# Moving the chunk borders of one token mixer and shortening two key blocks of the other, in a fused decoder block

## The chip, the cores and the metric

One core of a Trainium2 chip. The core has a matrix engine (TensorE, PE in the profile; its weight loads are PEld), a vector engine (DVE), an activation engine (ACT), GpSimd (POOL) and a queue engine for transfers (SP). The metric is device time in microseconds (us), the median of several runs; less is better.

## The reference

One decoder block on 16 learned meta tokens followed by 512 real tokens, model width 1024, 4 heads. All in float32. After a norm, one input projection feeds two token mixers that run side by side:

- Mixer 1 (mLSTM). Queries and keys go through a causal convolution and SiLU. Row j of the output is a sum over keys s <= j of exp(d[j,s]) (q_j . k_s) v_s, with d from running sums of gate logs, stabilised by a row maximum and divided by a normaliser.
- Mixer 2 (gated linear attention). A state S is carried over time, S_t = diag(alpha_t) S_(t-1) + k_t v_t^T, and o_t = S_t^T q_t, with a decay per key channel.

Each head's output is normed and gated, the two mixers are merged by sigmoid gates and projected, and a SwiGLU channel mixer follows. The meta rows are dropped at the end:

```
q_dec = q * exp(bc);  k_inv = k * exp(-bc);  k_end = k * exp(btot - bc)
att   = where(causal, q_dec @ k_inv.T, 0);   intra = att @ v
S_new = exp(btot)[:, None] * S + k_end.T @ v
out   = intra + q_dec @ S_prev               # per chunk; bc restarts in each
```

The chunk length is a choice of the implementation: any borders give the same sums.

## The kernel before

Activations lie transposed, channels on the 128 partitions and time along the free axis: 528 columns, the 16 meta tokens first. Weights come from memory in units of 128x1024 by the SP queue (some halves by POOL), through a ring of four raw buffers.

**fp32 by three fp32r products.** A float32 operand is split on chip into a high part rounded to fp32r (ACT, `whi`, L190) and the rest (DVE, `wlo`, L195), and a product becomes three: high x high, high x low, low x high (`mm3`, L304 to L306). The same is done for mixer 1's q, k, values and weights. Some projections are done in pairs by a seven-product scheme on 2x2 blocks (`seven`, L346 to L348), with additions on ACT and DVE in `sink_of` (L407 to L415). Mixer 2's own products are plain fp32: one instruction in the program, two records in the trace.

**Order.** The program writes the order of every engine's instructions by hand. `JOBS` lists the projection units. After each step of a unit (or every second one in a paired unit) `tick()` advances small generators, which issue the evacuations, the splits and the mixers' work between the products; `yield n` means "again in n ticks". One mixer head runs at a time. Each engine carries out its instructions in that order and waits when an operand is not there. Work tiles come from one pool of 60 buffers (`NTT`), PSUM tiles from 8 banks.

**Chunks.** Both mixers cut time into five windows of `CH` = 128 tokens that start with the meta tokens: the first holds 16 meta and 112 real tokens, the last only 16 real ones (`jrange`, `kwin`).

**Mixer 1, per head** (`mlstm`). For each key block i of the five, all queries from the block's first one on are scored at once, so that the blocks are 512, 400, 272, 144 and 16 queries wide: three fp32r products (L918 to L920) into a PSUM bank, an exponential on ACT, their product on DVE (L925), then a split of the result into `wh` (ACT, L935) and `wl` (DVE, L938) and a running sum (L942). Afterwards, for each of two 128-wide value halves, three products per block (L960 to L962) are accumulated into `num`. `values` first transposes v by TensorE (L755, L773), copies the result to a high part (L759, L776) and subtracts for a low part (L764, L781). `conv_act` makes the q and k splits (L737, L739).

**Mixer 2, per head** (`gla_decay`, `gla`, with `values` again, here without a low part). A running sum of the decay's logs, restarted at chunk borders by a 0/1 row `rmask` (L1006), gives the scaled q and k. Then four key windows are transposed (L1039), five score products are made (L1047), masked on DVE (L1050), eight products build the chunk states (L1058), ACT and DVE chain them (L1066 to L1071), and eighteen products give the output (L1079, L1081): ten with the masked scores, eight with the states.

`gate_rows` makes the gate logs and transposes them in 32-row pieces (L703). The epilogue of each head is `head_out`.

Of the kernel before, what the change touches and what calls it, by code (L numbers as in the profile page):

```python
# [15 lines left out]
P = 128  # L16
# [13 lines left out]
NCK = 5  # L30

# [71 lines left out]
def hybrid_block(ctx: ExitStack, tc: tile.TileContext, xT, wst, par, con, out):  # L103
# [526 lines left out]
    def gate_rows(ps):  # L630
# [45 lines left out]
        selector(0)  # L676

# [46 lines left out]
    def conv_act(q, k, src):  # L724
# [9 lines left out]
        for b, a in ((q, src[0].v), (k, src[1].v)):  # L734
            n = a.shape[1]
            hi, lo = tt(F32R, n), tt(F32R, n)
            act(hi, a, AF.Copy, scale=0.5)  # L737
            yield 2
            V.scalar_tensor_tensor(lo, a, 0.5, hi.bitcast(F32), ALU.mult, ALU.subtract)  # L739
            b.v = hi, lo  # L740
# [3 lines left out]
    def values(box, tail, vf, h, need_lo):  # L744
        dt = F32R if need_lo else F32
        full = []
        ps = []
        for vt in range(2):
            while vf[vt].v is None:
                yield 1  # L750
            yield 8 if h or not need_lo else 16
            f = vf[vt].v
            pb = bank()
            for c in range(4):
                T.transpose(pb[:, c * P:(c + 1) * P], f[:, c * CH:(c + 1) * CH], ident)  # L755
            yield 1
            ps.append(pb)
            a = tt(dt, NS)
            S.copy(a, pb)  # L759
            b = None  # L760
            yield 1
            if need_lo:
                b = tt(F32R, NS)
                V.tensor_tensor(b, pb, a.bitcast(F32), ALU.subtract)  # L764
            full.append((a, b))
            yield 1
        if h % 2 == 0:
            tail[0] = tt(dt, NS)
            tail[1] = tt(F32R, NS) if need_lo else None
        o = 256 * (h % 2)  # L770
        pb = bank()
        for vt in range(2):
            T.transpose(pb[:, vt * P:(vt + 1) * P], vf[vt].v[:, NT - CH:NT], ident)  # L773
        yield 1
        ta = tail[0][:, o:o + 256]
        S.copy(ta, pb[:, :256])  # L776
        tb = None
        yield 1
        if need_lo:
            tb = tail[1][:, o:o + 256]  # L780
            V.tensor_tensor(tb, pb[:, :256], ta.bitcast(F32), ALU.subtract)  # L781

        def pick(j):
            def f(c, vt):
                return full[vt][j][:, c * P:(c + 1) * P] if c < NCK - 1 else (ta, tb)[j][:, vt * P:(vt + 1) * P]
# [93 lines left out]
    WTOT = off  # L879
# [6 lines left out]
    def mlstm(h, q, k, v, gates, dst):  # L886
        while not gts.ready or q.v is None or k.v is None:
            yield 1
        (qh, ql), (kh, kl) = q.v, k.v
# [21 lines left out]
        for i in range(NCK + 1):  # L911
            cur = None
            if i < NCK:
# [3 lines left out]
                sp = bank()[:, :n]  # L917
                T.matmul(sp, kh[:, w0:w1], qh[:, j0:], start=True, stop=False)  # L918
                T.matmul(sp, kh[:, w0:w1], ql[:, j0:], start=False, stop=False)
                T.matmul(sp, kl[:, w0:w1], qh[:, j0:], start=False, stop=True)  # L920
                e = tt(n=n)
                cur = sp, e, WOFF[i], n
                act(e[:, :j1 - j0], dia[:, j0:j1], AF.Exp, bias=col(0, i))
            if prev:
                V.tensor_tensor(prev[1], prev[0], prev[1], ALU.mult)  # L925
            yield 1
# [6 lines left out]
            if prev:  # L933
                p, e_, o, m = prev
                S.copy(wh[:, o:o + m], e_)  # L935
            yield 1
            if prev:
                V.tensor_tensor(wl[:, o:o + m], e_, wh[:, o:o + m].bitcast(F32), ALU.subtract)  # L938
# [16 lines left out]
        for vt in range(2):  # L955
            for i in range(NCK):
                j0, o = jrange(i)[0], WOFF[i]
                n = NS - j0
                fi, la = i == 0, i == NCK - 1
                T.matmul(num[vt][:, j0:], vh(i, vt), wh[:, o:o + n], start=fi, stop=False)  # L960
                T.matmul(num[vt][:, j0:], vh(i, vt), wl[:, o:o + n], start=False, stop=False)  # L961
                T.matmul(num[vt][:, j0:], vl(i, vt), wh[:, o:o + n], start=False, stop=la)  # L962
# [17 lines left out]
    def gla_decay(h, gq, gk, dk):  # L980
# [27 lines left out]
        mid = CH // 2 - 1  # L1008
        c4 = 4 * CH
        v4 = lambda a: a[:, :c4].rearrange("p (a b) -> p a b", a=4)  # L1010
        V.tensor_tensor(v4(b3), v4(bc), v4(bc)[:, :, mid:mid + 1].to_broadcast([P, 4, CH]), ALU.subtract)
        V.tensor_scalar(b3[:, c4:], bc[:, c4:], bc[:, c4 + 7:c4 + 8], None, op0=ALU.subtract)
        ex = apool.tile([P, 3, 8], F32, tag="ex", name=nm("ex"), bufs=2)
# [8 lines left out]
        act(ex[:, 2, :4], b3[:, CH - 1:c4:CH], AF.Exp, scale=-1.0 / TAU)  # L1022
# [9 lines left out]
    def gla(h, dk, v, gates, dst):  # L1032
# [5 lines left out]
        for c in range(4):  # L1038
            T.transpose(pk[:, c * P:(c + 1) * P], ki[:, CH * c:CH * c + CH], ident)  # L1039
# [4 lines left out]
        for c in range(NCK):  # L1044
            j0, j1 = jrange(c)
            w0, w1 = kwin(c)
            T.matmul(ap_[:, j0:j1], ki[:, w0:w1], qd[:, j0:j1], start=True, stop=True)  # L1047
# [8 lines left out]
        for c in range(4):  # L1056
            for vt in range(2):
                T.matmul(Us[c // 2][:, 256 * (c % 2) + vt * P:256 * (c % 2) + (vt + 1) * P],  # L1058
                         kit[:, c * P:(c + 1) * P], gv(c, vt), start=True, stop=True)
            yield 1  # L1060
        Sv = None
        Sps = []
        for c in range(4):
# [7 lines left out]
            V.tensor_scalar(Sp, Sv, ex[:, 1, c + 1:c + 2], None, op0=ALU.mult)  # L1071
# [4 lines left out]
        for c in range(NCK):  # L1076
            j0, j1 = jrange(c)
            for vt in range(2):
                T.matmul(o[vt][:, j0:j1], gv(c, vt), att[:, j0:j1], start=True, stop=c == 0)  # L1079
                if c > 0:  # L1080
                    T.matmul(o[vt][:, j0:j1], Sps[c - 1][:, vt * P:(vt + 1) * P], qd[:, j0:j1],  # L1081
                             start=False, stop=True)
            yield 1
        yield 1
# [461 lines left out]
def _pack(inputs):  # L1546
# [63 lines left out]
    con[:, K_M01:K_M01 + NS] = keep  # L1610
# [21 lines left out]
```

## Time and profile before

| what | value |
|---|---|
| time, median of 3 runs | 938.07 us (938.03 to 938.1) |
| profiled execution: span, first to last instruction | 937.5 us |
| mean granted TensorE clock in it | 0.997 |
| TensorE busy, instructions | 914.6 us (98%), 6083 |
| DVE busy | 637.0 us (68%) |
| ACT busy | 536.2 us (57%) |
| POOL busy | 87.2 us (9%) |
| moved by transfers | 124.46 MB |

The page gives the profiled execution's span; the time of a run also holds what lies around the first and the last instruction, and here the median is 0.57 us above the span. A line of the page such as `L305 PE MATMUL b<-t,whi 128*128 128x512 f32` names the source line, the engine, the operation, the tile written and the tiles read, and the shapes: weights of 128x128, 512 columns streamed. In the timeline a row begins with the start and the duration in us, and ends with the count of instructions merged into it and, in brackets, how long the engine stood idle before it and what it waited for. Durations of products overlap, since a product starts while the one before it is still draining.

### The profile page before, as it was taken

The numbers are of one execution on the slowest core, as the hardware profiler recorded it, in microseconds if no ns is written. First come the engines' busy times: TensorE is split into PE (matmuls) and PEld (weight loads), VectorE is DVE, ScalarE is ACT, GpSimd is POOL, SyncE is SP. The second block draws the span as 40 slices with busy tenths as digits, with TensorE's granted clock in tenths as the row PEclk, the third lists the DMA queues.
The fourth block names the chain that finished last, engine by engine and source line by source line (L and its number), as shares of the span: only waits on it lengthen the run. The fifth ranks groups of instructions, "written<-read, shape, count | busy, mean of one in ns | idle before, by whom it ended". The sixth has DMA issues, their size and how long they took to land.

```text
span 937.5 us, 15478 instructions
## 1 busy us (share of the span) xinstructions
PE 914.6 (98%) x6083; PEld 839.7 (90%) x6083; DVE 637.0 (68%) x938; ACT 536.2 (57%) x956; POOL 87.2 (9%) x103
## 2 busy tenths in 40 slices
PE   6999999999999999999999999999999999999995
PEld 6988999989998899999998888889999999888885
DVE  6888886778865577777777556886676776932323
ACT  7666677888774166867674234443555555732322
POOL 0000022011100011111000000212111210000000
PEclk9999999999999999999999999999999999999998
DMA  6335475354652466565552344245777676332302
GB/s 254 114 115 165 141 167 123 71 141 110 159 155 90 113 162 162 133 135 142 123 147 90 113 139 134 87 121 116 192 174 201 176 180 169 114 104 76 113 1 90
DMA packets 48713, 124.46 MB, mean 133 GB/s; under 512 B 5376, under 2 KB 11520, under 8 KB 48640
## 3 DMA queue, kind: packets, MB, share of 16 engines
q1 hardware_dynamic: 35008, 101.32, 34.0%
q0 software_dynamic: 12544, 21.11, 14.6%
q8 instruction: 47, 0.77, 0.3%
q10 hardware_dynamic: 1088, 1.05, 0.3%
q14 instruction: 26, 0.21, 0.1%
HBM read 118.08 MB, written 5.37 MB: 132 GB/s over the span
## 4 chain that ended last, share of the span: by engine, by line
PE 84%; DVE 7%; ACT 6%; issue 2%; DMA 1%; SPq 0%; DVEq 0%; ACTq 0%
PE b L304 15%; PE b L305 15%; PE b L306 14%; PE b L346 11%; PE b L348 11%; PE b L347 11%; ACT t L134 2%; DVE wlo L195 2%; ACT whi L190 2%; PE b L1079 1%; DMA t<-xT 1%; PE b L1081 1%; PE b L1058 1%; ACT L133 1%; PE b L961 1%
## 5 line engine op out<-in xcount | busy, mean ns | idle before, releaser
L305 PE MATMUL b<-t,whi 128*128 128x512 f32 (+2 forms) x822 | 290.2, 353 | 1.3 <-DVE t L474 0.7
L304 PE MATMUL b<-t,whi 128*128 128x512 f32 (+2 forms) x774 | 273.9, 354 | 6.7 <-ACT t L134 6.7
L306 PE MATMUL b<-t,wlo 128*128 128x512 f32 (+2 forms) x774 | 270.9, 350 | 0.0
L195 DVE TENSOR_TENSOR wlo<-raw,whi 128x1024 fp32r<-128x1024 f32 x155 | 193.9, 1254 | 97.4 <-ACT whi L190 97.0
L346 PE MATMUL b<-t,whi 128*128 128x256 f32 (+1 forms) x864 | 248.7, 288 | 2.5 <-ACT t L407 1.2
L348 PE MATMUL b<-t,wlo 128*128 128x256 f32 (+1 forms) x864 | 244.5, 283 | 0.9 <-DVE wlo L195 0.9
L347 PE MATMUL b<-t,whi 128*128 128x256 f32 (+1 forms) x864 | 243.8, 282 | 0.0
L190 ACT CAST whi<-raw 128x1024 fp32r<-128x1024 f32 x155 | 161.9, 1048 | 55.2 <-PE b L347 22.7
L305 PEld LDWEIGHTS b<-t,whi 128*128 128x128 f32 x822 | 155.7, 189 | 24.1 <-DVE t L474 1.7
L304 PEld LDWEIGHTS b<-t,whi 128*128 128x128 f32 x774 | 146.9, 190 | 26.4 <-ACT t L134 6.7
L346 PEld LDWEIGHTS b<-t,whi 128*128 128x128 f32 x864 | 163.0, 189 | 3.7 <-ACT t L408 1.6
L306 PEld LDWEIGHTS b<-t,wlo 128*128 128x128 f32 x774 | 146.7, 190 | 20.0 <-DVE wlo L195 0.4
L348 PEld LDWEIGHTS b<-t,wlo 128*128 128x128 f32 x864 | 162.7, 188 | 1.7 <-DVE wlo L195 1.5
L347 PEld LDWEIGHTS b<-t,whi 128*128 128x128 f32 x864 | 163.0, 189 | 0.4
L134 ACT ACTIVATE t<-t 128x512 f32<-128x512 f32 (+6 forms) x140 | 80.4, 594 | 57.2 <-DVE t L1108 27.8
L185 POOL DMA_DIRECT2D raw<-wst x36 | 31.1, 864 | 361.7 <-DMA wf<-wst 94.0
L190 ACT CAST whi<-wf 128x1024 fp32r<-128x1024 f32 x36 | 37.8, 1049 | 22.4 <-PE b L347 12.6
L214 POOL DMA_DIRECT2D wf<-wst x36 | 34.8, 966 | 153.2 <-DMA wf<-wst 79.8
L134 ACT ACTIVATE t<-f 128x256 f32<-128x256 f32 (+1 forms) x24 | 11.6, 481 | 61.7 <-DVE f L1479 61.7
L195 DVE TENSOR_TENSOR wlo<-wf,whi 128x1024 fp32r<-128x1024 f32 x36 | 43.9, 1219 | 0.0
L1479 DVE TENSOR_TENSOR f<-f,b 128x512 f32<-128x512 f32 (+1 forms) x9 | 5.7, 629 | 53.8 <-PE b L306 53.8
L1401 ACT COPY t<-b 128x256 f32<-128x256 f32 x48 | 16.4, 374 | 44.3 <-PE b L348 44.3
(221 smaller groups left out, 1225.6 us busy)
## 6 DMA issues: line engine op xcount, KB each, us to landing
raw<-wst SPq DMA_DIRECT2D x155, 512.0 KB, 3.7
wf<-wst SPq DMA_DIRECT2D x36, 256.0 KB, 3.5
wf<-wst POOLq DMA_DIRECT2D x36, 256.0 KB, 5.9
raw<-wst POOLq DMA_DIRECT2D x36, 256.0 KB, 4.2
t<-xT SPq DMA_DIRECT2D x8, 264.0 KB, 6.9
pos<-t SPq DMA_DIRECT2D x8, 264.0 KB, 2.5
t<-xT SPq DMA_DIRECT2D x8, 256.0 KB, 3.9
t<-neg POOLq DMA_DIRECT2D x6, 272.0 KB, 6.4
```

Of the source, the lines that this page charges most:

```text
L134: S.activation(o, i, func, **kw)
L185: G.dma_start(lr(r, 0), lr(wst[v - 1], 0), accum_op=ALU.add)
L190: S.copy(t, src)
L195: V.tensor_tensor(t, src, hi.bitcast(F32), ALU.subtract)
L214: G.dma_start(lr(st.f, 1), lr(wst[u + 1], 1), accum_op=ALU.add)
L304: T.matmul(o, w_h, ah[:, c0:c1], start=first, stop=False)
L305: T.matmul(o, w_h, al[:, c0:c1], start=False, stop=False)
L306: T.matmul(o, w_l, ah[:, c0:c1], start=False, stop=last)
L346: T.matmul(o, h, xh_[k][:, c0:c1], start=start and k == 0, stop=False, skip_group_check=not start)
L347: T.matmul(o, h, xl_[k][:, c0:c1], start=False, stop=False, skip_group_check=not start)
L348: T.matmul(o, l, xh_[k][:, c0:c1], start=False, stop=k == 3, skip_group_check=not start)
L1401: s7=lambda: S.copy(s[:, lo], bz), s1=lambda: S.copy(s[:, hi], bx), s2=lambda: S.copy(r[:, lo], bx),
```

## The change

Mixer 2 gets chunk borders after the 16 meta tokens: one chunk of 16 meta keys, which have no real queries and only give a first state, and four chunks of 128 real tokens. Its values are transposed in windows that begin at token 16, plus one window of 16 meta tokens for both value halves, which lands on 16 partitions. The first state is one product with 16 rows and 256 columns; the scores are four products of 128 columns, the output sixteen (each of eight blocks by its scores and by its state). `rmask` is rewritten for these borders behind its last use by mixer 1's gates, and the mask of mixer 2 becomes four triangles.

Mixer 1 keeps its windows. Its last two key blocks (144 and 16 queries) are scored by one fp32 product each of the unsplit q and k, into one shared PSUM bank; their weights are not split, and each goes into `num` by one fp32 product with unsplit values. The first three blocks stay as they were. The unsplit q and k are twice the split ones, so a factor 0.25 is put into the DVE product.

```diff
+NWH = 3
@@ gate_rows
         selector(0)
+        G.memset(rmask[:, CH:NT:CH], 1.0)
+        G.memset(rmask[:, NM:NS:CH], 0.0)
@@ conv_act
-            b.v = hi, lo
+            b.v = hi, lo, a
@@ values
+        nw, w = (NWH, 0) if need_lo else (4, NM)
+        rest = [(c, vt) + kwin(c) for c in range(nw, NCK) for vt in range(2)] if need_lo else [
+            (None, vt, 0, NM) for vt in range(2)]
+        m = rest[0][3] - rest[0][2]
-            for c in range(4):
-                T.transpose(pb[:, c * P:(c + 1) * P], f[:, c * CH:(c + 1) * CH], ident)
+            for c in range(nw):
+                T.transpose(pb[:, c * P:(c + 1) * P], f[:, w + c * CH:w + (c + 1) * CH], ident)
-            a = tt(dt, NS)
-            S.copy(a, pb)
+            a = tt(dt, nw * P)
+            S.copy(a, pb[:, :nw * P])
-                V.tensor_tensor(b, pb, a.bitcast(F32), ALU.subtract)
+                V.tensor_tensor(b, pb[:, :nw * P], a.bitcast(F32), ALU.subtract)
-        for vt in range(2):
-            T.transpose(pb[:, vt * P:(vt + 1) * P], vf[vt].v[:, NT - CH:NT], ident)
+        for i, (c, vt, w0, w1) in enumerate(rest):
+            T.transpose(pb[:m, i * P:(i + 1) * P], vf[vt].v[:, w0:w1], ident)
-        S.copy(ta, pb[:, :256])
-        if need_lo:
-            V.tensor_tensor(tb, pb[:, :256], ta.bitcast(F32), ALU.subtract)
+        S.copy(ta, pb[:m, :n])
@@ mlstm
+                if i < NWH:
                     ...
+                else:
+                    if i == NWH:
+                        spn, en = bank(), tt()
+                    c = slice(WOFF[i] - WTOT, WOFF[i] - WTOT + n)
+                    sp, e = spn[:, c], en[:, c]
+                    T.matmul(sp, kf[:, w0:w1], qf[:, j0:], start=True, stop=True)
+            elif prev:
+                V.scalar_tensor_tensor(prev[1], prev[0], 0.25, prev[1], ALU.mult, ALU.mult)
+                if o < WTOT:
+                    S.copy(wh[:, o:o + m], e_)
+                if o < WTOT:
+                    V.tensor_tensor(wl[:, o:o + m], e_, wh[:, o:o + m].bitcast(F32), ALU.subtract)
+                if i >= NWH:
+                    T.matmul(num[vt][:, j0:], vh(i, vt), en[:, o - WTOT:o - WTOT + n], start=False, stop=i == NCK - 1)
+                    continue
@@ gla_decay
-        mid = CH // 2 - 1
+        mid = NM + CH // 2 - 1
     ...
-        act(ex[:, 0, :4], bc[:, CH - 1:c4:CH], AF.Exp, scale=-1.0 / TAU)
-        act(ex[:, 1, :4], bc[:, mid:c4:CH], AF.Exp, scale=-1.0 / TAU)
-        act(ex[:, 1, 4:5], bc[:, c4 + 7:c4 + 8], AF.Exp, scale=-1.0 / TAU)
+        act(ex[:, 0, 1:], bc[:, NM + CH - 1:NT - CH:CH], AF.Exp, scale=-1.0 / TAU)
+        act(ex[:, 1], bc[:, mid:NT:CH], AF.Exp, scale=-1.0 / TAU)
@@ gla
-            T.transpose(pk[:, c * P:(c + 1) * P], ki[:, CH * c:CH * c + CH], ident)
+            w = max(0, NM + CH * (c - 1))
+            T.transpose(pk[:, c * P:(c + 1) * P], ki[:, w:w + CH], ident)
-        for c in range(NCK):
-            T.matmul(ap_[:, j0:j1], ki[:, w0:w1], qd[:, j0:j1], start=True, stop=True)
+        for c in range(4):
+            T.matmul(ap_[:, blk(c)], ki[:, NM + CH * c:NM + CH * c + CH], qd[:, blk(c)], start=True, stop=True)
-        for c in range(4):
+        T.matmul(Us[0][:, :256], kit[:NM, :P], gv(None, 0), start=True, stop=True)
+        for c in range(3):
             for vt in range(2):
-                T.matmul(Us[c // 2][:, 256 * (c % 2) + vt * P:256 * (c % 2) + (vt + 1) * P],
-                         kit[:, c * P:(c + 1) * P], gv(c, vt), start=True, stop=True)
+                o = 256 * ((c + 1) % 2) + vt * P
+                T.matmul(Us[(c + 1) // 2][:, o:o + P], kit[:, (c + 1) * P:(c + 2) * P], gv(c, vt), start=True, stop=True)
-        for c in range(NCK):
+        for c in range(4):
             for vt in range(2):
-                T.matmul(o[vt][:, j0:j1], gv(c, vt), att[:, j0:j1], start=True, stop=c == 0)
-                if c > 0:
-                    T.matmul(o[vt][:, j0:j1], Sps[c - 1][:, vt * P:(vt + 1) * P], qd[:, j0:j1],
-                             start=False, stop=True)
+                T.matmul(o[vt][:, blk(c)], gv(c, vt), att[:, blk(c)], start=True, stop=False)
+                T.matmul(o[vt][:, blk(c)], Sps[c][:, vt * P:(vt + 1) * P], qd[:, blk(c)], start=False, stop=True)
```

The counts of `yield` along each path are the same as before, so everything keeps its place in the order of the ticks.

More of the change, by code (lines that the diff above doesn't have):

```diff
@@ L762, in values @@
             if need_lo:
-                b = tt(F32R, NS)
-                V.tensor_tensor(b, pb, a.bitcast(F32), ALU.subtract)
+                b = tt(F32R, nw * P)
+                V.tensor_tensor(b, pb[:, :nw * P], a.bitcast(F32), ALU.subtract)
             full.append((a, b))
             yield 1
[L767 to L770, printed above, removed]
+        n = len(rest) * P
+        if need_lo or h % 2 == 0:
+            tail[0] = tt(n=NS)
+        o = 0 if need_lo else n * (h % 2)
         pb = bank()
-        for vt in range(2):
-            T.transpose(pb[:, vt * P:(vt + 1) * P], vf[vt].v[:, NT - CH:NT], ident)
+        for i, (c, vt, w0, w1) in enumerate(rest):
+            T.transpose(pb[:m, i * P:(i + 1) * P], vf[vt].v[:, w0:w1], ident)
         yield 1
-        ta = tail[0][:, o:o + 256]
-        S.copy(ta, pb[:, :256])
-        tb = None
+        ta = tail[0][:m, o:o + n]
+        S.copy(ta, pb[:m, :n])
         yield 1
-        if need_lo:
-            tb = tail[1][:, o:o + 256]
-            V.tensor_tensor(tb, pb[:, :256], ta.bitcast(F32), ALU.subtract)
+        at = {r[:2]: i * P for i, r in enumerate(rest)}
         def pick(j):
             def f(c, vt):
-                return full[vt][j][:, c * P:(c + 1) * P] if c < NCK - 1 else (ta, tb)[j][:, vt * P:(vt + 1) * P]
+                if c is None:
+                    return ta
+                if (c, vt) in at:
+                    return ta[:, at[c, vt]:at[c, vt] + P]
+                return full[vt][j][:, c * P:(c + 1) * P]
             return f
@@ L878, in hybrid_block @@
         off += NS - jrange(i)[0]
-    WTOT = off
+    WTOT = WOFF[NWH]
     def selector(h):
@@ L888, in mlstm @@
             yield 1
-        (qh, ql), (kh, kl) = q.v, k.v
+        (qh, ql, qf), (kh, kl, kf) = q.v, k.v
         yield 6
@@ L916, in mlstm @@
                 n = NS - j0
[L917 to L921, printed above, removed]
+                if i < NWH:
+                    sp = bank()[:, :n]
+                    T.matmul(sp, kh[:, w0:w1], qh[:, j0:], start=True, stop=False)
+                    T.matmul(sp, kh[:, w0:w1], ql[:, j0:], start=False, stop=False)
+                    T.matmul(sp, kl[:, w0:w1], qh[:, j0:], start=False, stop=True)
+                    e = tt(n=n)
+                else:
[4 more added lines that the diff above has]
+                    T.matmul(sp, kf[:, w0:w1], qf[:, j0:], start=True, stop=True)
                 cur = sp, e, WOFF[i], n
                 act(e[:, :j1 - j0], dia[:, j0:j1], AF.Exp, bias=col(0, i))
-            if prev:
+            if prev and i <= NWH:
                 V.tensor_tensor(prev[1], prev[0], prev[1], ALU.mult)
+            elif prev:
+                V.scalar_tensor_tensor(prev[1], prev[0], 0.25, prev[1], ALU.mult, ALU.mult)
             yield 1
@@ L1609, in _pack @@
     con[:, K_MADD:K_MADD + NS] = np.where(keep, 0.0, -1e30)
-    con[:, K_M01:K_M01 + NS] = keep
+    con[:, K_M01:K_M01 + NS] = np.arange(P)[:, None] <= np.arange(NS)[None, :] % CH
     for h in range(H):
```

28 lines of the change are left out of this document (11 added, 17 removed).

## The prediction

> **What bounds the kernel now.** I read the page first (busy times, then the chain of work that ended last), then TensorE's own waits in order of time, then the instructions of the two mixers product by product.
>
> ```profile
> span 937.5 us, 15478 instructions
> PE 914.6 (98%) x6083; PEld 839.7 (90%) x6083; DVE 637.0 (68%) x938; ACT 536.2 (57%) x956; POOL 87.2 (9%) x103
> PE 84%; DVE 7%; ACT 6%; issue 2%; DMA 1%; SPq 0%; DVEq 0%; ACTq 0%
> ```
>
> TensorE (PE) is busy for 914.6 of 937.5 us, and 84% of the chain that ended last is its own work. So the time moves by what the change takes from or adds to TensorE, unless it makes TensorE wait. The timeline of TensorE has only a handful of waits between its first product and its last; the four inside mixer 1 that bear on the change (the bracket gives the idle time and what ended it):
>
> ```profile
> 73.32 0.50 PE L918 MATMUL b<-t,t 128*128 128x512 f32 x1 [0.63 <-DVE t L764]
> 102.77 0.47 PE L960 MATMUL b<-wh,t 128*128 128x512 f32 x1 [0.31 <-DVE t L764]
> 207.27 0.39 PE L346 MATMUL b<-t,whi 128*128 128x256 f32 x1 [1.24 <-ACT t L407]
> 213.13 0.39 PE L346 MATMUL b<-t,whi 128*128 128x256 f32 x1 [1.06 <-ACT t L408]
> ```
>
> What a product costs TensorE must be read from how far apart products start; the durations in the rows overlap.
>
> **Part A: mixer 1, key blocks 3 and 4 (144 and 16 queries wide) as single fp32 products.** There are three such groups per head: the scores, and the value product for each of the two value halves. Each was two blocks of three fp32r products. The tail of one value product in head 0, and the projection behind it:
>
> ```profile
> 99.70 0.23 PE L960 MATMUL b<-wh,t 128*128 128x144 f32 x1
> 99.76 0.28 PE L961 MATMUL b<-wl,t 128*128 128x144 f32 x1
> 99.87 0.27 PE L962 MATMUL b<-wh,t 128*128 128x144 f32 x1
> 99.99 0.22 PE L960 MATMUL b<-wh,t 128*128 128x16 f32 x1
> 100.06 0.26 PE L961 MATMUL b<-wl,t 128*128 128x16 f32 x1
> 100.17 0.26 PE L962 MATMUL b<-wh,t 128*128 128x16 f32 x1
> 100.28 0.37 PE L304 MATMUL b<-t,whi 128*128 128x264 f32 x1
> 100.49 0.28 PE L305 MATMUL b<-t,whi 128*128 128x264 f32 x1
> ```
>
> From 99.70 to the second projection product at 100.49 are 0.79 us. One 264-wide product takes 0.12 in a dense run (60.65 to 60.77 for the same form, below), so the six narrow ones cost 0.67, or 0.11 each, and 16 columns cost as much as 144. What is paid is not the columns but one load of 128x128 weights per product.
>
> Next, what a single fp32 product costs. In the trace one fp32 product is two records. Four 16-wide fp32 products of mixer 2 in a row (two rows left out), and the projection behind them:
>
> ```profile
> 289.45 0.29 PE L1079 MATMUL b<-t,t 128*128 128x16 f32 x2
> ...
> 290.04 0.38 PE L1081 MATMUL b<-t,Sp 128*128 128x16 f32 x2
> 290.26 0.48 PE L304 MATMUL b<-t,whi 128*128 128x512 f32 x1
> 290.58 0.39 PE L305 MATMUL b<-t,whi 128*128 128x512 f32 x1
> 290.81 0.40 PE L306 MATMUL b<-t,wlo 128*128 128x512 f32 x1
> ```
>
> 290.58 - 289.45 is 1.13; less 0.23 for one 512-wide product it is 0.90 for four, 0.22 each: two loads at 0.11. Up to 128 columns the price is the same, as L1058 in the chain of waits shows: two 128-wide products (four records) in 0.45. L1500 there prices a wide product, and L755 the transposes of part C:
>
> ```profile
> 85.66 0.44 PE b L755 x4
> ...
> 270.42 0.45 PE b L1058 x4
> ...
> 916.50 0.43 PE b L1500 x2
> ```
>
> L1500 is one fp32 product 256 wide: 0.43. Its columns are the cost there, so 144 columns take 0.43 x 144/256 = 0.24. A group of 0.67 becomes 0.24 + 0.22 = 0.46 and saves 0.21. Twelve groups: **-2.5 us**. The bounds: six loads against four alone (0.67 - 0.44) would give 0.23 per group, -2.8; if the 144-wide one cost as much as the 256-wide, 0.02, or -0.2.
>
> The Trainium skill speaks against this part: FP8 and Floating Point Precision, TensorE Precision Notes, has true fp32 make four passes through the array, and three fp32r products are three. By passes alone a group would rise from 3 x 160 to 4 x 160 columns, at 0.12/264 us a column 0.07 us more, and part A would be +0.9 instead of -2.5. The rows show the four passes on wide products (0.43 for 256 columns against 0.12 for 264 in fp32r) but a floor per load on narrow ones, so I take the rows.
>
> With part A also go, per head, the splits of blocks 3 and 4 on ACT (L935) and DVE (L938), one DVE split of the values' tail (L781) and a quarter of the two others (L764). They are off TensorE's path except at the waits above; see part D.
>
> **Part B: mixer 2 with four full blocks.** Scores go from 5 products to 4, the output from 18 to 16. Removed are three narrow fp32 products per head (widening 112 to 128 columns is free, as the load is the price): 3 x 0.22 x 4 heads = **-2.7 us**. The price is measured in this very form; were only the columns paid, it would be 3 x 0.03 x 4, -0.3, the upper bound.
>
> **Part C: what the 16 meta keys cost.** The state of the meta chunk is one fp32 product with 16 rows and 256 columns in place of two 128-wide ones: 0.43 against 0.44, equal. Two of the ten value transposes per head now have 16 columns instead of 128; they cost 0.11 (L755 above, four in 0.44). But both kinds use only a corner of the array, and the trace has one such place, the gate transposes with 32 rows. One of them, then (from another window) five in a row:
>
> ```profile
> 60.65 0.28 PE L305 MATMUL b<-t,whi 128*128 128x264 f32 x1
> 60.77 0.28 PE L306 MATMUL b<-t,wlo 128*128 128x264 f32 x1
> 60.98 0.24 PE L703 MATMUL b<-pr,t 32*128 32x32 f32 x1
> 61.15 0.39 PE L304 MATMUL b<-t,whi 128*128 128x264 f32 x1
> 61.38 0.29 PE L305 MATMUL b<-t,whi 128*128 128x264 f32 x1
> ```
>
> ```profile
> 55.75 0.28 PE L306 MATMUL b<-t,wlo 128*128 128x264 f32 x1
> 55.96 0.49 PE L703 MATMUL b<-pr,t 32*128 32x32 f32 x5
> 56.61 0.28 PE L305 MATMUL b<-t,whi 128*128 128x264 f32 x1
> ```
>
> 60.77 to 61.38 is 0.61; less two wide products (0.24) one transpose costs 0.37. With five it is 0.86 - 0.24 = 0.62. Four more cost 0.25, 0.06 each, so 0.31 us is the price of going into the small form and out again: the load of the next weights is not started until the work before it has ended.
>
> The Trainium skill has the rule: TensorEngine Tiling (Array Packing), Tiling Modes, Key Properties, says that "Mode switching requires drain", and lists both 32 rows and 32 columns as modes. The row agrees for rows; no row shows columns.
>
> Per head: the 16-row product enters and leaves once, +0.31 - 0.01 = +0.30; the two narrow transposes (adjacent) once, +0.31, their own price left at 0.11. I take both, as L703 is the only narrow form there is: 4 x 0.61 = **+2.4 us**. Bounds: below, no break for either and 0.06 per transpose, -0.06 - 0.4 = -0.5; above, twice the break (0.62, if the wide fp32 product or a full array drains longer than a 32-wide one), +4.9.
>
> **Part D: the waits.** L764 now writes 384 columns instead of 512. By form:
>
> ```profile
> L764 DVE TENSOR_TENSOR t<-b,t 128x512 fp32r<-128x512 f32 x8 | 5.5, 688 | 5.2 <-ACT t L759 5.2
> L938 DVE TENSOR_TENSOR wl<-t,wh 128x400 fp32r<-128x400 f32 x4 | 2.3, 575 | 5.2 <-ACT wh L935 5.2
> ```
>
> 113 ns for 112 columns, so 128 columns are 0.13: the waits at 73.32 and 102.77 shorten by 0.13 each, **-0.3** (0 if TensorE's earlier work, not DVE's length, set them). Before the wait at 213.13 ACT does this:
>
> ```profile
> 211.46 1.15 ACT L134 ACTIVATE t<-t 128x512 f32<-128x512 f32 x2
> 212.51 0.29 ACT L935 CAST wh<-t 128x144 fp32r<-128x144 f32 x1
> 212.71 0.36 ACT L408 COPY t<-b 128x256 f32<-128x256 f32 x1
> ```
>
> L935 for block 3 is gone, L408 comes 0.2 earlier. But head 3's score group saves its 0.2 between the two ACT waits and only waits longer: **0** in sum.
>
> Costed at nothing: the two strided memsets on POOL (used 9%; the next reader is mixer 2), the block 3 evacuation that now shares a PSUM bank with block 4 (DVE's product for block 3 is issued behind block 4's scores anyway), the ACT copy of the tail (512 columns instead of 256, but the two copies ahead of it are 128 shorter each). If that cover were gone, each would cost at most one instruction of 0.2 to 0.6 us per head. No DMA is added or moved.
>
> **Sum**: -2.5 - 2.7 + 2.4 - 0.3 = -3.1; as parts A and B lose a little where ACT or DVE lead (head 3's 0.2 is already out), I take **-2.9**. Span 937.5 - 2.9 = 934.6. The median of the runs shown is 938.07, 0.57 above the span; **935.2 us**.
>
> **Rivals.** *No break* (932.3 to 934): if neither narrow form breaks the run, part C is -0.5 and the sum -2.5 - 2.7 - 0.5 - 0.3 = -6.0, 932.1; if only the transposes don't, -4.2, 933.9. For: 32 output columns are unseen. Against: L703.
>
> *Swallowed* (937.3): ACT, not TensorE, is the bound up to 213 us, and what part A saves before it (all but the two value groups of head 3, 10/12 of 2.5 = 2.1) becomes longer waits at 207 and 213: -2.9 + 2.1 = -0.8. For and against stand in ACT's rows:
>
> ```profile
> 190.13 0.37 ACT L776 CAST t<-b 128x256 fp32r<-128x256 f32 x1 [1.57 <-PE b L773]
> 193.50 0.37 ACT L410 COPY t<-b 128x256 f32<-128x256 f32 x1 [0.17 <-PE b L348]
> ```
>
> Only 0.17 us of slack at 193.50, but 1.57 before 190.13, ended by TensorE: if TensorE is early there, so is ACT. The weights' splits could still lag.
>
> *Four passes* (938.5): part A as +0.9; sum +0.9 - 2.7 + 2.4 - 0.3 = +0.3. Needs the floor per load not to hold, which the six products contradict.
>
> *Slower: buffers.* The pool of work tiles has 60 buffers. The unsplit q and k, so far free once their low parts are made, must now live until block 4's scores, and the weights of blocks 3 and 4 until the last value product. For head 3:
>
> ```profile
> 176.15 0.70 DVE L739 SCALAR_TENSOR_TENSOR t<-t,t 128x528 fp32r<-128x528 f32 x1
> 208.23 0.26 PE L920 MATMUL b<-t,t 128*128 128x16 f32 x1
> ```
>
> That is 208.5 instead of 176.9, 32 us with two buffers fewer. If the pool runs out, an ACT instruction between 193 and 208 stands still until 208.5, with the projection's copies and splits behind it; one that is due at 204.1 (ACT's gate functions start there) waits 4.4 us, and TensorE with it: 935.2 + 4.4 = 939.6. With the same in one more head, 944.0. It decides from 2.9 + 1.9 = 4.8 us of added waits. Against: no wait in the trace can be named as one for a buffer, and the values' tail takes one buffer less per head pair.
>
> **Chances.** What a measurement of this kernel can tell from no change is about 0.2%, 1.9 us. Forecast 0.50, no break 0.18, swallowed 0.18, four passes 0.05, buffers 0.09. Faster by over 0.2% (below 936.2): the first two, 0.68. Within: 0.23. Slower: 0.09. The range 932.4 to 938.0 leaves out the lowest end of *no break* and the slower cases.
>
> **What would show it.** In the profile after: the TensorE records of blocks 3 and 4 as four loads in 0.46 us; TensorE's busy time about 3 us lower; a gap of 0.1 us before and 0.2 behind the 16-row product and the narrow transposes, or none (then 932 to 934); the waits at 207 and 213 of the old size. Wrong would be: waits of TensorE on ACT or DVE in heads 1 to 3 longer by more than 1 us, or single fp32 products that start over 0.3 us apart.

## The result, and the profile after

| | before | after |
|---|---|---|
| time, median | 938.09 us (938.03 to 938.54) | 933.33 us (933.12 to 933.61) |
| profiled execution: span | 937.5 us | 931.8 us |
| TensorE busy, instructions | 914.6 us, 6083 | 910.6 us, 6027 |
| DVE busy | 637.0 us | 633.5 us |
| ACT busy | 536.2 us | 534.0 us |

The ratio of the times is 0.9947, 95% interval 0.9935 to 0.9959: the changed kernel is faster by 4.8 us. The forecast was 935.2 in a range from 932.4 to 938.0. The spans differ by 5.7 us, more than the times: in all later runs the time is 1.7 to 2.1 us above the span, while the kernel before's median is only 0.57 above the span of its profiled execution, so that this execution was itself, as far as these gaps tell, some 1.2 us longer than the median. That excess lies ahead of the mixers: the product behind TensorE's wait near 70 us starts at 70.00 us there and between 68.22 and 68.95 in the traces of all the other runs. Effects are therefore compared below by the times, or within one stage.

From the page of the kernel after: span, busy times, and the shares of the chain that ended last.

```profile
span 931.8 us, 15342 instructions
PE 910.6 (98%) x6027; PEld 834.4 (90%) x6027; DVE 633.5 (68%) x926; ACT 534.0 (57%) x944; POOL 87.2 (9%) x105
PE 83%; DVE 8%; ACT 6%; issue 2%; DMA 1%; SPq 0%; DVEq 0%; ACTq 0%
```

TensorE has 56 records fewer and is busy 4.0 us less; the bound has not moved. Line numbers have: `mm3` is L305 to L307 now, `seven` L347 to L349, mixer 1's scores L925 to L927 and L934, its value products L980 to L982 and L978.

A single fp32 group in head 0 (one value half's two last blocks; four records in one row), with what stands before and behind it, from TensorE's timeline after:

```profile
97.46 0.29 PE L982 MATMUL b<-wh,t 128*128 128x272 f32 x1
97.58 0.54 PE L978 MATMUL b<-t,t 128*128 128x144 f32 x4
97.97 0.37 PE L305 MATMUL b<-t,whi 128*128 128x264 f32 x1
98.18 0.28 PE L306 MATMUL b<-t,whi 128*128 128x264 f32 x1
```

98.18 - 97.58 is 0.60; less one 264-wide product (0.12) the group costs 0.48. Predicted were 0.46 after 0.67. The 144-wide product by itself stands among the scores of head 1:

```profile
122.93 0.28 PE L307 MATMUL b<-t,wlo 128*128 128x264 f32 x1
123.05 0.41 PE L934 MATMUL b<-t,t 128*128 128x144 f32 x2
123.20 0.38 PE L305 MATMUL b<-t,whi 128*128 128x264 f32 x1
123.42 0.29 PE L306 MATMUL b<-t,whi 128*128 128x264 f32 x1
```

123.42 - 123.05 less 0.12 is 0.25, where the prediction had 0.24 by its columns.

The two narrow transposes of a head's values (L778, 16 columns), same view:

```profile
260.65 0.28 PE L349 MATMUL b<-t,wlo 128*128 128x256 f32 x1
260.77 0.38 PE L778 MATMUL b<-pr,t 128*16 128x128 f32 x2
260.91 0.36 PE L347 MATMUL b<-t,whi 128*128 128x256 f32 x1
261.11 0.28 PE L348 MATMUL b<-t,whi 128*128 128x256 f32 x1
```

They start without a gap, 0.12 behind the product before them, and 261.11 - 260.77 less one 256-wide product (0.12) leaves 0.22 for two. There is no break.

The 16-row product (L1074) and the two 128-wide ones behind it (L1078):

```profile
265.13 0.28 PE L349 MATMUL b<-t,wlo 128*128 128x256 f32 x1
265.34 0.69 PE L1074 MATMUL b<-t,t 16*128 16x256 f32 x2
265.96 0.71 PE L1078 MATMUL b<-t,t 128*128 128x128 f32 x4
266.43 0.37 PE L347 MATMUL b<-t,whi 128*128 128x256 f32 x1
```

Here the run is broken: 0.21 from the product before to L1074 where dense products stand 0.12 apart, then 0.62 where a 256-wide fp32 product takes 0.43. The break is there for the 16-row product and not for the transposes with 16 columns. The weight loads (PEld) say the same: the load for the transposes starts 0.10 us ahead of its product (260.77), while behind the 16-row product the next load starts only with its own product, after 0.33 us without any:

```profile
260.67 0.19 PEld L778 LDWEIGHTS b<-pr,t 128*16 128x16 f32 x2
265.96 0.52 PEld L1078 LDWEIGHTS b<-t,t 128*128 128x128 f32 x4 [0.33 <-issue]
```

Not every form with fewer rows breaks the run. Two products with 96 rows start 0.13 us behind the one at 210.94, and the next follows at 211.31, 0.12 for each:

```profile
211.07 0.41 PE L1010 MATMUL b<-t,a2s 96*128 96x264 f32 x2
```

Mixer 2's output, 16 single fp32 products in place of 18 (first and last, and the projection behind):

```profile
280.95 0.38 PE L1098 MATMUL b<-t,t 128*128 128x128 f32 x2
...
282.50 0.39 PE L1099 MATMUL b<-t,Sp 128*128 128x128 f32 x2
282.65 0.48 PE L305 MATMUL b<-h,whi 128*128 128x512 f32 x1
282.97 0.40 PE L306 MATMUL b<-t,whi 128*128 128x512 f32 x1
```

282.97 - 280.95 less 0.23 is 1.79 for the eight shown, 0.22 each at 128 columns, the price that 16 columns had before.

The waits of TensorE in mixer 1, first the one of the kernel before that the prediction did not show, then those over 0.2 us of the kernel after:

```profile
70.00 0.50 PE L894 MATMUL b<-t,sel 128*128 128x512 f32 x1 [1.07 <-ACT acol L697]
```

```profile
68.94 0.50 PE L900 MATMUL b<-t,sel 128*128 128x512 f32 x1 [0.85 <-ACT acol L700]
100.88 0.47 PE L980 MATMUL b<-wh,t 128*128 128x512 f32 x1 [0.73 <-DVE t L769]
191.18 0.39 PE L349 MATMUL b<-t,wlo 128*128 128x256 f32 x1 [0.34 <-DVE wlo L196]
203.33 0.38 PE L347 MATMUL b<-t,whi 128*128 128x256 f32 x1 [0.57 <-ACT t L408]
208.78 0.38 PE L347 MATMUL b<-t,whi 128*128 128x256 f32 x1 [0.72 <-ACT t L409]
```

Before, they sum to 4.31 us (1.07 and the four in the prediction), after to 3.21. The wait ahead of head 0's first score product (73.32 before) is gone, that at 207.27 has halved, that at 213.13 lost a third, and a new one of 0.34 has come. The wait near 70 us differs from trace to trace, whatever the kernel (0.57 to 1.07 in the others), so its 0.2 is not put down to the change.

### The profile page after: what moved, and what is told of

It is laid out like the page before. It is cut to its first block, busy times and chain, and to the rows that moved or that the text cites. A ratio compares the mean times of both kernels' runs of the same rounds, so it can differ in the third digit from the quotient of the medians.

```text
span 931.8 us, 15342 instructions
## 1 busy us (share of the span) xinstructions
PE 910.6 (98%) x6027; PEld 834.4 (90%) x6027; DVE 633.5 (68%) x926; ACT 534.0 (57%) x944; POOL 87.2 (9%) x105
## 4 chain that ended last, share of the span: by engine, by line
PE 83%; DVE 8%; ACT 6%; issue 2%; DMA 1%; SPq 0%; DVEq 0%; ACTq 0%
PE b L305 14%; PE b L306 14%; PE b L307 14%; PE b L349 12%; PE b L347 12%; PE b L348 12%; ACT t L135 3%; DVE wlo L196 2%; ACT whi L191 2%; DMA t<-xT 1%; PE b L1099 1%; PE b L1098 1%; PE b L1078 1%; ACT L134 1%; PE b L761 1%
## 5 line engine op out<-in xcount | busy, mean ns | idle before, releaser
L305 PE MATMUL b<-t,whi 128*128 128x512 f32 (+2 forms) x774 | 274.1, 354 | 6.6 <-ACT t L135 6.6
L307 PE MATMUL b<-t,wlo 128*128 128x512 f32 (+2 forms) x774 | 270.8, 350 | 0.0
L347 PE MATMUL b<-t,whi 128*128 128x256 f32 (+1 forms) x864 | 248.5, 288 | 1.6 <-ACT t L409 1.0
L349 PE MATMUL b<-t,wlo 128*128 128x256 f32 (+1 forms) x864 | 244.7, 283 | 0.8 <-DVE wlo L196 0.8
L305 PEld LDWEIGHTS b<-t,whi 128*128 128x128 f32 x774 | 146.7, 190 | 26.1 <-ACT t L135 6.6
L347 PEld LDWEIGHTS b<-t,whi 128*128 128x128 f32 x864 | 163.2, 189 | 3.0 <-ACT t L409 1.7
L307 PEld LDWEIGHTS b<-t,wlo 128*128 128x128 f32 x774 | 146.6, 189 | 20.0 <-DVE wlo L196 0.3
L349 PEld LDWEIGHTS b<-t,wlo 128*128 128x128 f32 x864 | 162.6, 188 | 1.5 <-DVE wlo L196 1.4
```

Of the source, the lines that this page charges most:

```text
L305: T.matmul(o, w_h, ah[:, c0:c1], start=first, stop=False)
L307: T.matmul(o, w_l, ah[:, c0:c1], start=False, stop=last)
L347: T.matmul(o, h, xh_[k][:, c0:c1], start=start and k == 0, stop=False, skip_group_check=not start)
L349: T.matmul(o, l, xh_[k][:, c0:c1], start=False, stop=k == 3, skip_group_check=not start)
```

## The experiments

Four runs take the change apart, four test single causes of what the prediction missed, two the part that buffers play. Kernels measured together share their runs of the kernel before: 938.24, 938.33 and 938.37 us.

**Each part alone.** `a_only` has mixer 1's part with mixer 2 as before: against the changed kernel, `gla_decay`, `gla` and the mask are those of before, and

```diff
-        G.memset(rmask[:, CH:NT:CH], 1.0)
-        G.memset(rmask[:, NM:NS:CH], 0.0)
-        nw, w = (NWH, 0) if need_lo else (4, NM)
-        rest = [(c, vt) + kwin(c) for c in range(nw, NCK) for vt in range(2)] if need_lo else [
-            (None, vt, 0, NM) for vt in range(2)]
+        nw, w = (NWH, 0) if need_lo else (4, 0)
+        rest = [(c, vt) + kwin(c) for c in range(nw, NCK) for vt in range(2)]
```

`b_only` is the reverse: against the kernel before, `gla_decay`, `gla` and the mask are the changed ones, mixer 2 calls a copy of the new `values`, and

```diff
+        G.memset(rmask[:, CH:NT:CH], 1.0)
+        G.memset(rmask[:, NM:NS:CH], 0.0)
-                run(values(b.v, gtail, b.vf, h, False))
+                run(values_new(b.v, gtail, b.vf, h, False))
```

> Mixer 1's part alone; mixer 2 keeps its five windows from the first token. Theory 1, as in the prediction with the sizes from the changed kernel's trace: twelve groups save 0.2 us of weight loads each (2.4), and the work taken from ACT and DVE shortens TensorE's waits in heads 0 and 3 by about 1: 3.4 us less than before, 934.7. Theory 2, only the loads count and the rest of the gain is the start of the run, whose first 17 us were 0.8 shorter in the changed kernel's trace: 2.4 less, 935.7. The summed TensorE waits between 65 and 215 us tell them apart: about 2.3 by theory 1, over 3 by theory 2.

> Mixer 2's part alone; mixer 1 keeps fifteen fp32r products per group and all its splits. Both parts independent: twelve narrow fp32 products fewer at 0.22 (2.7), less four breaks at the 16-row product of 0.27 (1.1), so 1.6 us less than before, 936.5. As the prediction had it, with a break at the narrow transposes too: 0.3 less, 937.8. If the part only pays together with the other one: no difference, 938.1.

Measured: `a_only` 934.77 us, ratio 0.9963 (0.9951 to 0.9976), that is -3.5; `b_only` 936.71 us, 0.9982 (0.9973 to 0.9991), that is -1.5. The two add up to -5.0 beside -4.8 for the whole, so the parts hardly touch each other, as far as intervals of about 1 us can tell. Mixer 1's part gives 1.2 us more than its loads (12 groups by 0.19 are 2.3). The waits that the expectation wanted summed are 3.17 us, and 4.31 before; its two figures, 2.3 and over 3, fit only without the wait near 70 us, where they are 2.39 and 3.24. So read they speak for theory 1, as the time does. In `b_only` the same waits sum to 4.23, about what they were before. Mixer 2's part gives about what its products give with one break per head instead of two (-2.7 + 1.5 = -1.2).

**The 16-row product on 128 rows.** `meta128` keeps the meta values in a tile of 128 rows that is zero below the 16, so that the product fills the array; nothing else is changed.

```diff
+        gts.meta = apool.tile([P, NS], F32, name="meta")
+        G.memset(gts.meta, 0.0)
-            tail[0] = tt(n=NS)
+            tail[0] = tt(n=NS) if need_lo else gts.meta
-                    return ta
+                    return tail[0][:, o:o + n]
-        T.matmul(Us[0][:, :256], kit[:NM, :P], gv(None, 0), start=True, stop=True)
+        T.matmul(Us[0][:, :256], kit[:, :P], gv(None, 0), start=True, stop=True)
```

> The changed kernel, but the 16 meta values lie in a tile whose other 112 rows were set to zero once, and the product for the first state uses all 128 rows. Theory 1, the small row form breaks TensorE's run: the product costs 0.43 instead of 0.62 + 0.1, so 0.27 us less in each of four heads, 1.1 in all: 932.2. Rival, the break comes from the 256-wide fp32 product itself: no difference, 933.3.

Measured: 932.27 us, ratio 0.9936 (0.9924 to 0.9949), 1.1 below the changed kernel, as theory 1 expected. The same place in its timeline:

```profile
264.71 0.28 PE L349 MATMUL b<-t,wlo 128*128 128x256 f32 x1
264.83 0.59 PE L1076 MATMUL b<-meta,t 128*128 128x256 f32 x2
265.26 0.61 PE L1080 MATMUL b<-t,t 128*128 128x128 f32 x4
265.62 0.37 PE L347 MATMUL b<-t,whi 128*128 128x256 f32 x1
```

From the product before to the projection behind are 0.91 us, where the 16-row form took 1.30 (265.13 to 266.43). The break costs 0.39 us, 0.09 ahead of the product, 0.19 on it and 0.11 behind it; four heads make 1.6. In the traces that gain is there behind the fourth of these products: TensorE's next wait, for L409, ends at 454.98 us in the changed kernel and at 453.08 here, 1.9 apart, of which 0.4 were there ahead of the first (265.13 and 264.71). Of these 1.5 us the times show 1.1, and their intervals do not tell the two apart. The width is the same in both, so it is the rows.

The Trainium skill, TensorEngine Tiling (Array Packing), Tiling Modes, Key Properties, has a change of tiling mode drain the array. By these rows there is such a break for a change of rows, at 0.39 us for going in and out.

**The narrow transposes on 128 columns.** `col128` transposes tokens 0 to 127 in place of the 16, and uses the first 16 rows of the result.

```diff
-            (None, vt, 0, NM) for vt in range(2)]
+            (None, vt, 0, CH) for vt in range(2)]
-                    return ta
+                    return ta[:NM]
```

> The changed kernel, but the two narrow transposes of mixer 2's values take 128 columns (tokens 0 to 127) in place of 16; of the result the first 16 rows are used, as before. Theory from the changed kernel's trace: two narrow transposes took 0.22 us together, no more than two of 128 columns, so nothing changes: 933.3, and 0.22 us again. Rival, as the prediction had it: a form that fills only a corner of the array breaks the run by 0.31 us per head, and 128 columns save it: 933.3 - 1.2 = 932.1.

Measured: 933.65 us, ratio 0.9951 (0.9939 to 0.9964), the time of the changed kernel within its interval. The rows:

```profile
260.27 0.28 PE L349 MATMUL b<-t,wlo 128*128 128x256 f32 x1
260.39 0.38 PE L778 MATMUL b<-pr,t 128*128 128x128 f32 x2
260.53 0.37 PE L347 MATMUL b<-t,whi 128*128 128x256 f32 x1
260.73 0.28 PE L348 MATMUL b<-t,whi 128*128 128x256 f32 x1
```

0.12 to the transposes and 0.34 from them to the second projection product, as with 16 columns to the hundredth. The prediction's break on columns falls, for these fp32 transposes; no run here has another kind of product with weights of 16 columns.

The Trainium skill, TensorEngine Tiling (Array Packing), Tiling Modes, lists modes with fewer columns too; these rows show none of its drain for 16 columns.

**The removed splits put back as dead work.** `dead_split` lets ACT and DVE split the weights of blocks 3 and 4 as before; the result is used nowhere (the tiles `wh` and `wl` are widened to hold it).

```diff
-                if o < WTOT:
-                    S.copy(wh[:, o:o + m], e_)
+                S.copy(wh[:, o:o + m], e_)
-                if o < WTOT:
-                    V.tensor_tensor(wl[:, o:o + m], e_, ...)
+                V.tensor_tensor(wl[:, o:o + m], e_, ...)
```

> The changed kernel, but ACT and DVE still split the weights of mixer 1's last two key blocks (four instructions per head, 0.31 + 0.21 us on ACT, 0.30 + 0.17 on DVE); nothing reads the halves. The products on TensorE are those of the changed kernel. If the relief of ACT and DVE is what shortened the waits in head 3: slower than the changed kernel by 0.5 to 1, about 934.1, with the waits at 203 and 208 us back near 1.2 and 1.1. If only the products count: 933.3, same waits as the changed kernel.

Measured: 934.10 us, ratio 0.9957 (0.9943 to 0.997), 0.8 above the changed kernel. Two of TensorE's waits have grown, from 0.73 and 0.72:

```profile
100.64 0.48 PE L979 MATMUL b<-wh,t 128*128 128x512 f32 x1 [1.04 <-DVE t L769]
208.80 0.39 PE L347 MATMUL b<-t,whi 128*128 128x256 f32 x1 [0.92 <-ACT t L409]
```

Together they grew by 0.5, less than the expectation had. So work taken from ACT and DVE was worth half a microsecond or somewhat more, though DVE is busy for only 68% of the span and ACT for 57%. The wait at 203 us hardly grew (0.63 after 0.57): that one shrank for another reason.

**The wait for a bank.** By the compiled program's map of the banks, which no trace shows, head 0's first score product wrote before into a PSUM bank that a DVE subtraction (L764) had read last, and now writes into one that ACT's copy of the values' tail (L781) has read last. The trace of before shows the wait ended by L764. `dead_tail` adds a DVE read of that tail.

```diff
@@ gate_rows
+        gts.dead = apool.tile([P, 256], F32, name="dead")
@@ values
         S.copy(ta, pb[:m, :n])
         yield 1
+        if need_lo:
+            V.tensor_tensor(gts.dead, pb[:, :256], ta[:, :256], ALU.subtract)
```

> The changed kernel, with one more DVE instruction per head: it subtracts the first 256 columns of the values' tail from the PSUM bank from which they came, as the low part of the tail was made before; the result is used nowhere, so the output is that of the changed kernel. Bank theory: TensorE's wait of 0.63 us at 73.32 us in the kernel before was for the PSUM bank of head 0's first score product, whose last reader was a DVE subtraction; without the tail's subtraction the product gets a bank that ACT had read last, some 1.4 us earlier, and the wait is gone (71.45 us, no idle time). With the dead subtraction the old bank is taken again: a wait of 0.4 to 0.7 us on DVE comes back ahead of that product, in head 0 alone, and the time is 933.3 + 0.5 = 933.8. Rival (as the prediction had it): the wait shrank because the values' subtraction is 0.13 us shorter and DVE had less to do; then the dead subtraction, which comes after that one, brings at most 0.1 us back: 933.4.

The product after, and with the dead read:

```profile
71.45 0.39 PE L925 MATMUL b<-t,t 128*128 128x512 f32 x1
```

```profile
71.76 0.50 PE L928 MATMUL b<-t,t 128*128 128x512 f32 x1 [0.50 <-DVE t L770]
```

The wait is back, as the bank theory had it. The added read itself comes only at 72.99 us, behind the product, so the wait is not for it but for the subtraction ahead of it (L770, 71.15 to 71.70), as before. But the time is 933.11 us, ratio 0.9946 (0.9933 to 0.996), not 933.8. The wait for the values' low part near 101 us (0.73 after) has gone from its timeline: counted from the product behind the wait near 70 us, DVE ends that subtraction at the same time in both, and TensorE, half a microsecond later by then, no longer meets it. Of the two waits in head 0 (0.63 + 0.31 before, 0 + 0.73 after, 0.50 + 0 here) only the sum counts; the change took 0.2 from it.

**One more buffer, in the kernel before.** Before the wait at 207.27, ACT had stood still. The row of the kernel before:

```profile
202.11 0.40 ACT L134 ACTIVATE t<-t,acol 128x128 f32<-128x128 f32 x1 [1.63 <-DVE t L825]
```

This exponential (head 3, third block) reads nothing from L825; its tile lies in a buffer that L825 had still to read. `before_p61` is the kernel before with `NTT = 61`.

```diff
-NTT = 60
+NTT = 61
```

> The kernel before with 61 buffers in the pool of work tiles in place of 60, nothing else. Buffer theory: before, ACT stood still for 1.63 us at 202.11 us because the tile that its exponential writes lay in a buffer that DVE L825 had still to read, and what is queued behind it (the copies L407 to L410) came late, so TensorE waited 1.24 us at 207.27. With 61 buffers that tile falls into a buffer that a TensorE product (L821, near 199.5 us) read last. The stand at 202 falls below 0.5 us, the wait of TensorE at 207 to 0.6 or less, and the time is 938.1 - 0.6 = 937.5. Rival: ACT's own work sets that wait, or the stand moves to the next buffer; then the wait stays above 1 us and the time is 938.1. A new map of buffers can move other waits by some tenths either way.

Measured: 937.31 us, ratio 0.999 (0.9981 to 0.9999), so 1.0 us less, with an interval that ends just short of no change. ACT no longer stands there, and of the two waits of TensorE at 207 and 213 only the second is left, 0.80 where it was 1.06:

```profile
198.77 0.40 ACT L134 ACTIVATE t<-t,acol 128x128 f32<-128x128 f32 x1
```

```profile
210.05 0.39 PE L346 MATMUL b<-t,whi 128*128 128x256 f32 x1 [0.80 <-ACT t L408]
```

These two waits fell by 1.5 us together. So there was a wait for a buffer in the kernel before, and 61 buffers are worth 1.0 us there; not all of it need be this one stand, as the wait of 0.31 near 103 us is gone from this trace too. The prediction said that no wait for a buffer could be named; the row with L825 names it.

**Only the last block as a single product.** `nwh4` was meant to price the 144-wide product alone.

```diff
-NWH = 3
+NWH = 4
```

> The changed kernel with only mixer 1's last key block (16 queries) as single fp32 products; the block of 144 queries has its split weights and three fp32r products again, the values their fourth window's low part. Load theory: three products of 144 columns at 0.11 us each (0.33) stand for one fp32 product at 0.24 to 0.26, so each of the 12 groups rises by 0.08, together +1.0 us, and the longer subtractions and splits on DVE and ACT give some 0.2 back in waits: 934.5. Rival (the other bound of the prediction, a 144-wide fp32 product as dear as a 256-wide one, 0.43): each group would fall by 0.10, together -1.2 us: 932.1.

Measured: 939.44 us, ratio 1.0018 (1.0009 to 1.0027), 6.1 above the changed kernel; neither theory is near. ACT's row, then TensorE's:

```profile
203.49 0.40 ACT L135 ACTIVATE t<-t,acol 128x128 f32<-128x128 f32 x1 [4.03 <-PE b L926]
```

```profile
203.17 0.28 PE L926 MATMUL b<-t,t 128*128 128x144 f32 x1
...
208.65 0.58 PE L347 MATMUL b<-t,whi 128*128 128x256 f32 x1 [2.77 <-ACT t L408]
209.02 0.42 PE L348 MATMUL b<-t,whi 128*128 128x256 f32 x1
209.24 0.41 PE L349 MATMUL b<-t,wlo 128*128 128x256 f32 x1
```

It is the same exponential. Its tile now lies, by the program's map of buffers, in that of q's low part, which in this kernel the fourth block's split product reads last (L926, 203.17). The trace shows only that the wait ends with L926; that product reads k's high part too, and the argument is the same for either. ACT stands for 4.03 us, the copies behind it come late, and TensorE waits 2.77. In the changed kernel the tile lies there too, but blocks 3 and 4 read the unsplit q and k, so the third block's product is the buffer's last reader:

```profile
197.84 0.29 PE L926 MATMUL b<-t,t 128*128 128x272 f32 x1
```

```profile
198.16 0.40 ACT L135 ACTIVATE t<-t,acol 128x128 f32<-128x128 f32 x1 [0.92 <-PE b L926]
```

A second cost follows in nwh4. After the wait the products start 0.21 us apart instead of 0.12. The stretch behind the wait and the next one; behind the length stand busy time and count of PE, PEld, DVE, ACT and POOL, then TensorE's granted clock, the DMA share and GB/s:

```profile
208.60:214.80 6.20, 6.16 (x29) 6.16 (x30) 5.29 (x11) 6.04 (x13) 0.87 (x1) 0.50 0.54 83
214.80:221.00 6.20, 6.20 (x52) 6.20 (x52) 6.12 (x13) 4.20 (x9) 0.00 (x0) 0.98 0.45 126
```

At half the clock 29 records pass in 6.20 us, where 52 pass in the next 6.20. In the eleven runs the mean granted clock was 0.992 to 0.994 in six (939.25 to 940.82 us) and 0.996 or 0.997 in five (938.77 to 939.44). The traced run is one of the six; if the others lose their clock at the same place, which the mean does not show, this part comes and goes and is worth some 1.4 us. That is less than the 2.8 us that the 23 missing records would take at 0.12 each; at the slower pace TensorE has no second wait behind this one, as it has in the other kernels. The rest is the waits and the dearer groups.

The Trainium skill, TensorE: Matmul & The Clock Gate, Part 1, has TensorE's clock halved after an idle window of about 3.4 us, on a window that runs freely. The halving is seen here, behind a shorter wait of 2.77 us; the free window would be a reason why it comes in some runs only.

**The same with one more buffer.** `nwh4_p61` is nwh4 with `NTT = 61`, `after_p61` the changed kernel with it.

> The changed kernel with only the block of 16 queries as single fp32 products (as in the run nwh4), and with 61 buffers in the pool in place of 60. In nwh4 the first exponential of head 3's third block waited 4.03 us on ACT, because its tile lay in the buffer of q's low part, which the fourth block's second product (203.17 us) was the last to read; TensorE then waited 2.77 us. Buffer theory: with 61 buffers that tile falls into a buffer that DVE L831 read last, as in the kernel before, where ACT stood 1.63 us. So the stand falls from 4.0 to about 1.6 us, TensorE's wait from 2.8 to about 1.2, the granted clock stays whole, and the time falls from 939.4 to the changed kernel's 933.3 plus 1.0 (the 12 groups at three products) plus 0.7 to 1.2 (waits as long as in the kernel before) = 935.2. Rival: three products per group, or the splits of the weights of the fourth block, cost the 6 us themselves; then it stays within 0.5 of 939.4.

> The changed kernel with 61 buffers in the pool in place of 60, nothing else. The tile of the same exponential still lies in the buffer of q's low part, whose last reader is now the third block's own product. Theory: ACT's stand of 0.92 us there is the wait for that product and stays, TensorE's waits stay, and the extra buffer brings nothing: 933.3 (within 0.4). Rival: buffers still set TensorE's waits at 203 and 209 us after the change; then they shrink by some 0.5 us and the time falls below 932.8.

Measured: `nwh4_p61` 936.25 us, ratio 0.9978 (0.9969 to 0.9987), 3.2 below nwh4, with the exponential and the wait behind it as the buffer theory has them:

```profile
199.63 0.40 ACT L135 ACTIVATE t<-t,acol 128x128 f32<-128x128 f32 x1 [1.47 <-DVE t L831]
```

```profile
204.79 0.39 PE L347 MATMUL b<-t,whi 128*128 128x256 f32 x1 [1.11 <-ACT t L408]
```

So about half of nwh4's loss, 3.2 of 6.1 us, was one buffer and what followed from it. What is left over the changed kernel, 2.9 us, is 1.0 more than expected; the wait at 101 us (1.21 against 0.73) holds half of that, and the rest was not tracked down. `after_p61` took 932.82 us, ratio 0.9939 (0.9927 to 0.9952): 0.5 below, a little outside what the theory allowed and at the rival's bound, but with the waits at 203 and 209 us unchanged (0.59 and 0.74). So buffers no longer set those, and the 0.5 us have no cause that is shown.

## Why the prediction was right, and where it was off

By its steps, against its profiled execution; the measured terms are of the kernel after.

- **Part A**, predicted -2.5. Right in mechanism and size: the group costs 0.48 in place of 0.67, twelve make -2.3. The floor per weight load held against the count of passes (0.22 for 16 columns, 0.25 for 144); the rival *four passes* is out.
- **Part B**, predicted -2.7. Right: the fp32 products are 0.22 each at 128 columns as at 16.
- **Part C**, predicted +2.4. Half of it failed: the step "the two narrow transposes (adjacent) once, +0.31" was taken from the L703 row and given to another form. In `32*128 32x32` the weights have 32 rows and all 128 columns, and the 32 columns are streamed ones; the transposes' weights, `128*16`, are narrow in columns alone. That term is zero (`col128`). L703 was not the only form with fewer rows, either: the 96 rows of L990 (L1010 after) were in the kernel before, without a break. The other half, the 16-row product, was right and under-sized: 0.39 in place of 0.31 (`meta128`). Part C was +1.5 (four times 0.39, less the 0.01 that the price of the product itself falls).
- **Part D**, predicted -0.3. Mis-sized: the waits of mixer 1 fell by 1.1. The wait near 70 us, which the prediction did not count, is 0.2 of this and differs from trace to trace. The two waits on L764 did not shrink by 0.13 each; one vanished with its bank and the other grew, together -0.2. The wait at 213 fell by 0.3 and not by nothing, and a new one of 0.3 came at 191. The largest share, 0.7 at 207, stood in the row that says L825 ended ACT's stand: 1.63 us before, 0.92 after, with the copies behind it that much earlier. The prediction argued only with ACT's slack at 190 and 193 us, and did not look at what ACT waited for at 202.
- **Sum** with measured terms: -2.3 - 2.7 + 1.5 - 1.1 = -4.6, beside -4.8 in the times. A wait further on that the prediction did not look at adds 0.2: the 0.65 us at 465.61 before, on DVE's split of weights (L195), are 0.27 (454.98) and 0.17 (460.30) after. Of the 1.9 us between forecast and result, the transposes are 1.2, the waits of mixer 1 0.8, that wait 0.2, and 0.2 is what the forecast held back from its own sum; the dearer break (0.3) and part A (0.2) go the other way. So two terms were missed on the same side, and that the forecast came no further off is in part luck: the mis-sized terms took 0.5 us back.

Of the rivals, *no break* came closest in its half form ("if only the transposes don't", 933.9; its own terms give 933.8). That is what the transposes did, and only the waits are missing from it. *Swallowed* went the other way: ACT did lead at 207 and 213, and the change took from its delay as well. *Buffers* is seen in this kernel only as ACT's 0.92 us at 198.16, shorter than the 1.63 before, but its mechanism is real: an ACT instruction between 193 and 208 us that stands still until a late score product has read its buffer is what `nwh4` shows, at 939.4 us. The prediction counted the buffers that the change holds longer, the unsplit q and k, and missed those that it lets go earlier, the split ones, last read by the third block's products instead of the fifth's.

What stays open: why TensorE waited 0.2 less at 70 us (the other traces have 0.57 to 1.07, `before_p61` 0.82 and `b_only` 1.07, so it need not be the change), half a microsecond of nwh4_p61, and the 0.5 us of after_p61.

## What to carry to other kernels

Price narrow products by what a weight load takes in the trace, and a narrow form by the axis on which its weights are narrow: a break measured on 32 rows says nothing of 16 columns. Where work tiles come from a full pool, ask of every stall which tile's buffer it is for and who reads that buffer last; a change that lets a buffer go earlier or later moves such a stall by microseconds, far from the place that was edited. Two waits of one engine can be one wait, even 29 us apart as in head 0: removing the first may only lengthen the second.

## What was not expected of the hardware

A product with 16 rows costs 0.39 us for going in and out of that form; fp32 transposes with 16 columns cost nothing extra (0.12 ahead of the two and 0.34 behind, the same as with 128). Behind an idle stretch of 2.77 us, with one of 0.64 us some 4 us ahead of it, TensorE ran at half its clock for the next 6.2 us in the traced run of `nwh4`. And a single buffer more in a pool of 60 was worth 1.0 us in the kernel before and 3.2 in `nwh4`.
